# Mixer B of a two-layer trunk: where the residual's gain and shift are applied, and which engine scales the softmax rows

## The chip, the cores and the metric

The kernel runs on one core of a Trainium2 chip. The metric is the device time of one execution in microseconds (us); a lower one is better. The core has five engines that work side by side and wait for each other through semaphores: TensorE (PE in the rows; its weight loads are PEld), VectorE (DVE), ScalarE (ACT), GpSimd (POOL) and SyncE (SP), which issues the large transfers here. TensorE writes its results to PSUM, eight banks of 128 x 512 float32, which VectorE and ScalarE read; everything else lies in SBUF.

## The reference, cut to what matters

256 tokens of width 1024 in float32 pass through two layers. Layer 0 has mixer A (an mLSTM), layer 1 has mixer B (attention); after each mixer comes a mixture of 16 experts. Each of the four sub-layers ends in a layer norm over the residual:

```python
x = layer_norm(ALPHA * x + gate * f(modulate(x)), ln_g, ln_b)
# mixer B
k, v = split(modulate(x, kv_shift, kv_scale) @ w_kv)
q = modulate(x, shift, scale) @ wq / 8
p = softmax(q @ k.T - slope[h] * distance, causal)     # 16 heads of width 64
y = (p @ v) @ wo
```

## The kernel before, in words

The Python code is traced once into straight-line programs, one for each engine. Where nothing pins the order, a list scheduler decides it at build time: the priority is the order of the code, and an instruction is placed when its inputs, its buffers and its engine are free by the scheduler's own model. At run time every engine runs its list in order, so an instruction that waits holds up all behind it.

**Norm.** The norm that ends the experts of layer 0 leaves in `xt` the normalised residual without gain and shift (`normalise`, L572 to L577). Mixer B's modulations fold gain and shift into their own coefficients, so keys, values and queries need no other form of it. The residual that is added after mixer B does need it, times ALPHA: `xt = xt * (ALPHA g) + ALPHA b`. Gain and shift are rows of 1024 values. `ln_bank` (L509 to L514) makes one half of a row, the same on all 128 partitions, with a matmul into a PSUM bank. In the kernel before, `ln_rows` (L503 to L507) copies the four banks, times ALPHA, to an SBUF tile `lnrow` on ScalarE, and `ln_affine` (L579 to L582) applies them with four GpSimd operations of 128 x 1024. The call stands behind the transposes for the queries (L1491, L1492).

**Mixer B** (L1403 to L1547). The weights come in tiles of 512 KB through a ring of SBUF slots; all their loads are issued on SP's queue in the order of the code, each waiting until its slot is free. Each tile is split into two parts for precision: a cast on ScalarE (L267) and a subtraction on VectorE (L268), into one of three buffers. The products then take three matmuls each (L276 to L278). The order is `k_part(0)`, the queries' transposes, `k_part(1)`, `q_part(0)`, scores 0 and 1, `v_part(0)`, attends and scores in turn, `q_part(1)`, attends 2 and 3, scores 4 and 5, `v_part(1)`, attends 4 and 5 with scores 6 and 7, the product with `wo`, attends 6 and 7. `scores(e)` (L1445 to L1467) handles two heads: matmuls into two `bankB`, the distance term and the row maxima on VectorE, four exponentials with their sums on ScalarE, a reciprocal on VectorE, and the scaling of the rows by it. Token tile t = 0 (128 x 128 for each head) is scaled on VectorE, token tile t = 1 (128 x 256) on GpSimd (L1466). `attend(e)` transposes the rows on TensorE into two `bankB`, copies them to SBUF on ScalarE (L1478) and multiplies them with the values (L1482).

`bankA` and `bankB` are pools of four PSUM banks each. `bankB` serves the scores, the attends' transposes, the norm's rows, and the sums of the modulation's coefficients. Those sums are background work: `pump` (L433) threads the products of `w_ada` (L396, L398: VectorE, 128 x 512 each) between the splits.

Behind mixer B come the residual's addition (L558, L559), the norm, the router and the experts of layer 1 (`moe`), whose weights stream through the same ring. `moe` applies its own gain and shift from PSUM rows at L1344 and L1345, in the form the change now uses in mixer B.

Of the kernel before, what the change touches and what calls it, by code (L numbers as in the profile page):

```python
# [9 lines left out]
F32 = mybir.dt.float32  # L10
# [3 lines left out]
AF = mybir.ActivationFunctionType  # L14
OP = mybir.AluOpType
# [3 lines left out]
P = 128  # L19
D = 1024  # L20
# [11 lines left out]
ALPHA = (2.0 * 2) ** 0.25  # L32
# [120 lines left out]
def body(tc, **aps):  # L153
    with ExitStack() as ctx:
        _body(ctx, tc, **aps)


def _body(ctx, tc, x, w_ada, a_w_in, a_wq, a_wk, a_wv, a_w_out, b_w_kv, b_wq, b_wo, moe_w_gate, moe_w_up,
          moe_w_down, pc, rows, cst, out):
    nc = tc.nc  # L160
    V, A, T = [Ordered(tc, e) for e in (nc.vector, nc.scalar, nc.tensor)]
    G = nc.gpsimd
# [10 lines left out]
    def bankA(name):  # L173
        return psA.tile([P, 512], F32, tag="A", name=name)

    def bankB(name):
        return psB.tile([P, 512], F32, tag="B", name=name)
# [3 lines left out]
    xt = keep.tile([P, NT, D], F32, name="xt")  # L181
# [74 lines left out]
    def cols(w, j, name):  # L256

        v = [piece(f"{name}_{i}", w[512 * i:512 * i + 512, 512 * j:512 * j + 512]) for i in range(2)]
        return lambda k: v[k // 4][:, k % 4:k % 4 + 2, :]
# [26 lines left out]
    def dense_cm(pool, w, ks, act, banks, name, part=None):  # L286

        for i in range(0, len(ks), 2):
            if part is not None and i not in part:
                continue  # L290
            pump()
            ws = split(pool, w(ks[i]), f"{name}{ks[i]}")
            for z in range(2):
                if z:
                    pump()
                block_cm(banks, ws[z], act(i + z), i + z == 0, i + z == len(ks) - 1)

    def dense_tm(pool, w, ks, act, banks, name):

        for i in range(0, len(ks), 2):  # L300
            pump()
            ws = split(pool, w(ks[i]), f"{name}{ks[i]}")
            for z in range(2):
                if z:
                    pump()
                for t in range(NT):
                    mm3(banks[t], act(i + z, t), ws[z], i + z == 0, i + z == len(ks) - 1)
# [195 lines left out]
    def ln_rows(ln, t, scale):  # L503
        for q in range(2):
            for h in range(2):
                A.activation(t[q][:, 512 * h:512 * h + 512], ln_bank(ln, q, h, bankB), AF.Copy, scale=scale)
        return t  # L507

    def ln_bank(ln, q, h, bank):  # L509

        pg = bank(f"lnps{ln}_{q}_{h}")
        r = 8 * q + 2 * ln + h
        T.matmul(pg, pick[:, r:r + 1].to_broadcast([P, P]), lnr, start=True, stop=True)
        return pg  # L514
# [10 lines left out]
    def modulated(src, emit, name):  # L525

        for k2 in range(KD // 2):
            pt = transposed(src, name, k2)
            for kk in range(2):
                emit(2 * k2 + kk, pt[:, 256 * kk:256 * kk + 256], k2 % 2)  # L530
# [7 lines left out]
    def affine_split(hi, lo, sc, sh, nm):  # L538
        def emit(k, ps, odd):
            t = small.tile([P, S], F32, tag="cv", name=f"{nm}{k}")  # L540
            affine(t, ps, sc, sh, k, odd)
            split_to(hi[:, k, :], lo[:, k, :], t)
        return emit
# [32 lines left out]
            return A.activation(xt[:, t, :], src[:, t, :], AF.Identity, bias=nb, scale=st[1])  # L576
        return V.tensor_scalar(xt[:, t, :], src[:, t, :], st[0], st[1], op0=OP.subtract, op1=OP.mult)  # L577

    def ln_affine(row):  # L579
        for t in range(NT):  # L580
            G.tensor_tensor(xt[:, t, :], xt[:, t, :], row[0], op=OP.mult)
            G.tensor_tensor(xt[:, t, :], xt[:, t, :], row[1], op=OP.add)  # L582


    actx = ExitStack()
# [819 lines left out]
    pbh = bctx.enter_context(tc.tile_pool(name="pbh", bufs=1, reuse_waits="tile"))  # L1405
# [25 lines left out]
    def v_part(i):  # L1431
        w = cols(b_w_kv, 2 + i, f"wv_{i}")
        banks = [bankA(f"bv{i}_{t}") for t in range(NT)]
        dense_tm(wsp, w, range(KD), lambda k, t: (kh[:, k, P * t:P * t + P], kl[:, k, P * t:P * t + P]), banks, f"bv{i}_")
        for t in range(NT):
            A.copy(vv[:, t, 512 * i:512 * i + 512], banks[t])

    def q_part(i):
        w = cols(b_wq, i, f"wq_{i}")
        banks = [bankA(f"bq{i}_{c}") for c in range(2)]  # L1440
        dense_cm(wsp, w, range(KD), lambda k: (qh[:, k, :], ql[:, k, :]), banks, f"bq{i}_")
        for c2 in range(2):
            V.tensor_scalar(qs[(2 * i + c2) % QZ], banks[c2].rearrange("p (a b) -> p a b", a=2), 0.125, None, op0=OP.mult)

    def scores(e):  # L1445

        q = qs[(e // 2) % QZ]
        sb = pb3.tile([P, 2, 384], F32, tag="sb", name=f"sb{e}")
        ps = [bankB(f"s{2 * e + par}") for par in range(2)]
        for t in range(NT):  # L1450
            for par in range(2):
                r = slice(64 * par, 64 * par + 64)
                T.matmul(ps[par][:, P * t:P * t + P + P * t], q[r, e % 2, P * t:P * t + P], kT[r, e, 0:P + P * t], start=True, stop=True)
        for par in range(2):
            V.scalar_tensor_tensor(sb[:, par, :], dist, -(2.0 ** (-8.0 * (2 * e + par + 1) / AH)), ps[par][:, 0:384],
                                   op0=OP.mult, op1=OP.add)
        mx = small.tile([P, NT, 2], F32, tag="mx", name=f"mx{e}")
        sm_ = small.tile([P, NT, 2], F32, tag="smx", name=f"smx{e}")
        parts = [(t, par, slice(P * t, P + S * t)) for t in range(NT) for par in range(2)]
        for t in range(NT):  # L1460
            V.tensor_reduce(mx[:, t, :], sb[:, :, P * t:P + S * t], axis=AX.X, op=OP.max, negate=True)
        for t, par, c in parts:
            A.activation(sb[:, par, c], sb[:, par, c], AF.Exp, bias=mx[:, t, par:par + 1], accum_out=sm_[:, t, par:par + 1])
        V.reciprocal(sm_, sm_)
        for t, par, c in parts:
            (G if t else V).tensor_scalar(sb[:, par, c], sb[:, par, c], sm_[:, t, par:par + 1], 0.0, op0=OP.mult, op1=OP.add)  # L1466
        return sb  # L1467

    def attend(e, sb, bank=bankA):
        po = bank(f"bo{e}")  # L1470
        pT = []
        for par in range(2):
            h = 2 * e + par
            pt = bankB(f"bp{h}")
            for i in range(3):
                T.transpose(pt[:, P * i:P * i + P], sb[:, par, P * i:P * i + P], ident)
            pT.append(work[0].tile([P, 384], F32, tag="pT", name=f"bpT{h}"))
            A.copy(pT[par], pt[:, 0:384])  # L1478
        for t in range(NT):
            for par in range(2):  # L1480
                h = 2 * e + par
                T.matmul(po[64 * par:64 * par + 64, P * t:S], vv[:, t, 64 * h:64 * h + 64], pT[par][:, S * t:S + P * t],  # L1482
                         start=(t == 0), stop=(t == NT - 1))
        A.copy(oh_[:, e, :], po[:, 0:S])
        V.tensor_tensor(ol_[:, e, :], po[:, 0:S], oh_[:, e, :].bitcast(F32), op=OP.subtract)
# [2 lines left out]
        queue((8, 9, 10, 11), RATE[2])  # L1488
        k_part(0)
    modulated(xt, affine_split(qh, ql, scq, shq, "affq"), "tq")  # L1490
    lnrow = pbh.tile([P, 2, D], F32, tag="oh", name="lnrow")  # L1491
    ln_affine(ln_rows(1, [lnrow[:, q, :] for q in range(2)], ALPHA))  # L1492
    oh_ = pbh.tile([P, KD, S], F32R, tag="oh", name="oh_")
    ol_ = pbh.tile([P, KD, S], F32R, name="ol_")
    k_part(1)
    q_part(0)
    sb = {}
    sb[0] = scores(0)
    sb[1] = scores(1)
    v_part(0)  # L1500
    attend(0, sb[0])
    sb[2] = scores(2)
    attend(1, sb[1])
    sb[3] = scores(3)
    q_part(1)
    ptq.close()
    attend(2, sb[2])
    attend(3, sb[3])
    sb[4] = scores(4)
    sb[5] = scores(5)  # L1510
    v_part(1)
    attend(4, sb[4])
    sb[6] = scores(6)
    attend(5, sb[5])
# [75 lines left out]
```

## Time and profile before

| | |
|---|---|
| Time, median of 3 runs | 930.84 us (929.8 to 932.74) |
| Profiled execution, its own time | 929.63 us |
| Span of that execution (first to last instruction) | 927.9 us |
| Granted TensorE clock, mean | 0.989 of full speed |
| Busy: TensorE, VectorE, ScalarE, GpSimd | 887.9, 529.0, 334.9, 30.4 us |
| Moved from HBM | 318.56 MB, 343 GB/s over the span |

Times in the rows are microseconds from the start of the span. A matmul's record overlaps the next one's, so a run of matmuls is read by the distance of their starts. An idle time in square brackets names what ended it.

### The profile page before, as it was taken

Reading aid. Unit: us, or ns where it says so; the run is one execution under the profiler, and the core shown is the slowest. Engines: PE = TensorE matmul, PEld = TensorE weight load, DVE = VectorE, ACT = ScalarE, POOL = GpSimd, SP = SyncE. Lnnn points to the kernel's source line nnn. Section 1 sums busy time; section 2 is a strip of 40 time slices with the busy share of each in tenths; the row PEclk is TensorE's granted clock in tenths of the full one; section 3 lists DMA queues with packets and bytes.
Section 4 is the critical chain, followed back from the end, with each engine's and each line's share of the span. In section 5 each row is a group of like instructions: output and inputs, shape, how many; then the busy total and the mean of one; then the engine's idle time right before and its main releaser. Section 6 shows DMA issues by size and latency. Waiting matters only on the chain.

```text
span 927.9 us, 13867 instructions
## 1 busy us (share of the span) xinstructions
PE 887.9 (96%) x5205; PEld 542.0 (58%) x5208; DVE 529.0 (57%) x1016; ACT 334.9 (36%) x558; POOL 30.4 (3%) x42
## 2 busy tenths in 40 slices
PE   9999999999999899999999888999988999999994
PEld 5876988886867544434343268887664343434332
DVE  2475985866868843233333289998876223334317
ACT  3466665466547311111111035565552111101120
POOL 0020000000000000000000004021100000000000
PEclk9999999999999999999999999999999999999998
DMA  9999795696986989999999999967986999999993
GB/s 331 383 377 405 225 306 181 212 399 209 352 299 213 393 339 406 407 407 406 407 407 407 383 403 370 340 225 225 374 322 254 404 407 407 407 407 407 407 399 124
DMA packets 174250, 318.56 MB, mean 343 GB/s; under 512 B 10144, under 2 KB 28224, under 8 KB 174176
## 3 DMA queue, kind: packets, MB, share of 16 engines
q1 hardware_dynamic: 174032, 317.40, 92.3%
q8 instruction: 43, 0.70, 0.3%
q14 instruction: 31, 0.25, 0.1%
q10 hardware_dynamic: 144, 0.20, 0.1%
HBM read 316.51 MB, written 1.05 MB: 342 GB/s over the span
## 4 chain that ended last, share of the span: by engine, by line
PE 37%; DMA 10%; DVE 6%; issue 1%; ACT 1%; DVEq 0%; ACTq 0%; SPq 0%
PE pg L135 8%; PE py L135 7%; PE pu L135 7%; DMA w<-in_moe_w_up_dram 4%; PE ga L135 3%; PE po L135 3%; DMA w<-in_moe_w_down_dram 2%; DVE adacc L398 1%; DMA w<-in_moe_w_gate_dram 1%; PE bo L1482 1%; DMA wq<-in_b_wq_dram 1%; DMA ada<-in_w_ada_dram 1%; PE by L276 1%; PE bv L276 1%; PE by L278 1%
## 5 line engine op out<-in xcount | busy, mean ns | idle before, releaser
L135 PE MATMUL py<-w,aT 128*64 128x512 f32 (+1 forms) x576 | 117.3, 547 | 1.8 <-DMA w<-in_moe_w_down_dram 1.8
L1247 DVE SCALAR_TENSOR_TENSOR yl<-py,wsl,yh 128x512 fp32r<-128x512 f32 x28 | 21.0, 750 | 171.4 <-ACT yh L1246 171.4
L135 PE MATMUL pu<-w,xe 128*64 128x512 f32 x512 | 118.5, 596 | 0.2 <-DMA w<-in_moe_w_up_dram 0.2
L135 PE MATMUL pg<-w,xe 128*64 128x512 f32 x512 | 116.1, 597 | 0.0
L398 DVE SCALAR_TENSOR_TENSOR adacc<-ada,pk,adacc 128x512 f32<-128x512 f32 x112 | 86.0, 777 | 0.8
L135 PEld LDWEIGHTS py<-w,aT 128*64 128x64 f32 x576 | 41.2, 137 | 73.5 <-issue 59.8
L135 PEld LDWEIGHTS pu<-w,xe 128*64 128x64 f32 x512 | 36.0, 137 | 67.3 <-issue 60.6
L135 PEld LDWEIGHTS pg<-w,xe 128*64 128x64 f32 x512 | 34.8, 137 | 63.9 <-issue 58.9
L1213 ACT COPY aT<-aT 128x512 f32<-128x512 f32 x16 | 9.4, 586 | 139.5 <-PE aT L135 139.5
L558 DVE TENSOR_TENSOR lntmpe<-po,gate 128x512 f32<-128x512 f32 x56 | 36.0, 683 | 41.1 <-PE po L135 41.1
L1246 ACT ACTIVATE yh<-py,wsl 128x512 fp32r<-128x512 f32 x28 | 19.2, 687 | 84.0 <-PE py L135 84.0
L536 ACT ACTIVATE xe<-ga,coef 128x256 f32<-128x256 f32 x32 | 16.1, 561 | 71.8 <-PE ga L135 71.8
L276 PE MATMUL z<-hh,wz 128*128 128x256 f32 x128 | 37.6, 294 | 0.0
L277 PE MATMUL z<-hl,wz 128*128 128x256 f32 x128 | 36.0, 281 | 0.0
L559 DVE TENSOR_TENSOR xt<-xt,lntmpe 128x512 f32<-128x512 f32 x56 | 36.0, 681 | 0.0
L278 PE MATMUL z<-hh,wz 128*128 128x256 f32 x128 | 35.9, 280 | 0.0
L135 PE MATMUL ga<-onehot,xh 128*128 128x256 f32 x128 | 31.6, 324 | 0.2
L1206 DVE TENSOR_TENSOR a<-a,pu 128x512 f32<-128x512 f32 x16 | 11.0, 688 | 36.1 <-PE pu L135 20.2
L135 PE MATMUL xm<-hh,win 128*128 128x256 f32 x144 | 28.8, 289 | 0.7 <-ACT hh L135 0.7
L135 PEld LDWEIGHTS ga<-onehot,xh 128*128 128x128 f32 x128 | 25.1, 222 | 6.0 <-DVE xt L559 4.1
L1201 ACT ACTIVATE a<-pg 128x512 f32<-128x512 f32 x16 | 9.6, 597 | 52.2 <-PE pg L135 52.2
L135 PE MATMUL ga<-onehot,xl 128*128 128x256 f32 x128 | 27.4, 280 | 0.0
(389 smaller groups left out, 1965.4 us busy)
## 6 DMA issues: line engine op xcount, KB each, us to landing
w<-in_moe_w_gate_dram SPq DMA_DIRECT2D x128, 512.0 KB, 10.2
w<-in_moe_w_up_dram SPq DMA_DIRECT2D x128, 512.0 KB, 10.2
w<-in_moe_w_down_dram SPq DMA_DIRECT2D x128, 512.0 KB, 10.2
ada<-in_w_ada_dram SPq DMA_DIRECT2D x112, 512.0 KB, 7.0
win<-in_a_w_in_dram SPq DMA_DIRECT2D x16, 512.0 KB, 8.4
wz<-in_a_w_in_dram SPq DMA_DIRECT2D x16, 512.0 KB, 5.8
wout<-in_a_w_out_dram SPq DMA_DIRECT2D x16, 512.0 KB, 6.8
wv<-in_a_wv_dram SPq DMA_DIRECT2D x8, 512.0 KB, 5.5
```

Source lines behind the costliest of these rows:

```text
L135: return self.tc.keep_in_program_order(f(*a, **kw))
L276: T.matmul(ps, l[0], r[0], start=start, stop=False, skip_group_check=True)
L277: T.matmul(ps, l[0], r[1], start=False, stop=False, skip_group_check=True)
L278: T.matmul(ps, l[1], r[0], start=False, stop=stop, skip_group_check=True)
L398: V.scalar_tensor_tensor(a, w[:, k, :], c, a, op0=OP.mult, op1=OP.add)
L536: A.activation(dst, ps, AF.Identity, bias=sh[:, k:k + 1], scale=sc[:, k:k + 1])
L558: V.tensor_tensor(tmp, y, gate[:, c], op=OP.mult)
L559: V.tensor_tensor(dst[:, t, c], dst[:, t, c], tmp, op=OP.add)
L1201: A.activation(a, pg, AF.Silu)
L1206: V.tensor_tensor(a, a, pu, op=OP.mult)
L1246: A.activation(yh, py, AF.Copy, scale=wsl[:, b:b + 1])
L1247: V.scalar_tensor_tensor(yl, py, wsl[:, b:b + 1], yh.bitcast(F32), op0=OP.mult, op1=OP.subtract)
```

## The change

In mixer B the residual's gain and shift are no longer copied to SBUF and applied on GpSimd. VectorE applies them straight from the PSUM banks, with eight operations of 128 x 512 in place of four of 128 x 1024; the factor ALPHA is taken in the same operations. This is done in two halves of the columns, the first behind `q_part(1)`, the second behind `v_part(1)`. The softmax rows of token tile t = 1 are scaled on ScalarE; those of t = 0 stay on VectorE, where the addition of 0.0 is dropped.

```diff
-    def ln_affine(row):
+    def ln_affine(h):
+
+        c = slice(512 * h, 512 * h + 512)
+        pg, pb_ = [ln_bank(1, q, h, bankB) for q in range(2)]
         for t in range(NT):
-            G.tensor_tensor(xt[:, t, :], xt[:, t, :], row[0], op=OP.mult)
-            G.tensor_tensor(xt[:, t, :], xt[:, t, :], row[1], op=OP.add)
+            V.scalar_tensor_tensor(xt[:, t, c], xt[:, t, c], ALPHA, pg, op0=OP.mult, op1=OP.mult)
+            V.scalar_tensor_tensor(xt[:, t, c], pb_, ALPHA, xt[:, t, c], op0=OP.mult, op1=OP.add)
...
         for t, par, c in parts:
-            (G if t else V).tensor_scalar(sb[:, par, c], sb[:, par, c], sm_[:, t, par:par + 1], 0.0, op0=OP.mult, op1=OP.add)
+            if t:
+                A.activation(sb[:, par, c], sb[:, par, c], AF.Copy, scale=sm_[:, t, par:par + 1])
+            else:
+                V.tensor_scalar(sb[:, par, c], sb[:, par, c], sm_[:, t, par:par + 1], None, op0=OP.mult)
...
     modulated(xt, affine_split(qh, ql, scq, shq, "affq"), "tq")
-    lnrow = pbh.tile([P, 2, D], F32, tag="oh", name="lnrow")
-    ln_affine(ln_rows(1, [lnrow[:, q, :] for q in range(2)], ALPHA))
     oh_ = pbh.tile([P, KD, S], F32R, tag="oh", name="oh_")
...
     q_part(1)
+    ln_affine(0)
     ptq.close()
...
     v_part(1)
+    ln_affine(1)
     attend(4, sb[4])
```

## Rows read from the trace of the kernel before

**Rows 1.** The page's first part: busy time, share, instructions of each engine.
```profile
PE 887.9 (96%) x5205; PEld 542.0 (58%) x5208; DVE 529.0 (57%) x1016; ACT 334.9 (36%) x558; POOL 30.4 (3%) x42
```

**Rows 2.** The chain that ended last, 690 to the end: start, length, what.
```profile
855.59 3.22 PE pg L135 x15
858.81 10.22 DMA w<-in_moe_w_up_dram
```

**Rows 3.** What SP's queue waited for, 697 to 720: total, times, longest.
```profile
SPq L226 <- PE pg L135: 15.9, 6, 13.0
```

**Rows 4.** What TensorE waited for, 552 to 686: total, times, longest.
```profile
PE bk L278 <- DVE bk L268: 2.5, 1, 2.5
PE s L1453 <- DVE qs L1443: 1.2, 1, 1.2
PE bo L1482 <- ACT bpT L1478: 0.8, 3, 0.3
```

**Rows 5.** Busy time by stretch: length, then PE, PEld, DVE, ACT, POOL, clock, DMA.
```profile
566.00:578.00 12.00, 10.28 (x79) 8.97 (x77) 12.00 (x8) 5.61 (x11) 10.72 (x4) 1.00 0.95 368
...
630.00:648.00 18.00, 18.00 (x98) 12.98 (x96) 16.05 (x29) 10.91 (x28) 3.41 (x4) 1.00 0.63 199
648.00:666.00 18.00, 17.66 (x94) 12.64 (x93) 16.35 (x29) 10.53 (x28) 2.42 (x4) 1.00 1.00 350
666.00:686.00 20.00, 19.88 (x110) 14.13 (x110) 14.32 (x33) 7.03 (x14) 0.00 (x0) 1.00 0.88 335
```

**Rows 6.** GpSimd's timeline at the norm: start, length, instruction, count.
```profile
566.28 5.67 POOL L581 TENSOR_TENSOR xt<-xt,lnrow 128x1024 f32<-128x1024 f32 x2 [411.85 <-ACT lnrow L506]
571.90 5.10 POOL L582 TENSOR_TENSOR xt<-xt,lnrow 128x1024 f32<-128x1024 f32 x2
```

**Rows 7.** VectorE's timeline around it and at the first queries.
```profile
563.63 1.40 DVE L398 SCALAR_TENSOR_TENSOR adacc<-ada,pk,adacc 128x512 f32<-128x512 f32 x2
564.96 0.74 DVE L273 TENSOR_TENSOR ql<-affq,qh 128x256 fp32r<-128x256 f32 x2
...
567.67 2.00 DVE L398 SCALAR_TENSOR_TENSOR adacc<-ada,pk,adacc 128x512 f32<-128x512 f32 x1
569.59 5.19 DVE L273 TENSOR_TENSOR ql<-affq,qh 128x256 fp32r<-128x256 f32 x2
574.71 2.84 DVE L398 SCALAR_TENSOR_TENSOR adacc<-ada,pk,adacc 128x512 f32<-128x512 f32 x1
577.47 1.21 DVE L268 TENSOR_TENSOR bk<-wk,bk 128x1024 fp32r<-128x1024 f32 x1
...
596.24 1.28 DVE L1443 TENSOR_SCALAR qs<-bq 128x512 f32<-128x512 f32 x2
```

**Rows 8.** TensorE's timeline: a norm's row among the keys; the queries' last matmul.
```profile
565.06 0.50 PE L513 MATMUL lnps<-lnr,pick 128*128 128x512 f32 x1
565.39 0.28 PE L276 MATMUL bk<-kh,bk 128*128 128x256 f32 x1
...
595.05 0.28 PE L278 MATMUL bq<-qh,bq 128*128 128x256 f32 x1
```

**Rows 9.** Line L1344's instructions: least, median, longest ns, first and last start.
```profile
L1344 DVE SCALAR_TENSOR_TENSOR xt<-xt,lnps x8: 674/678/681, 325.5 to 707.6; 128x512 f32<-128x512 f32 x8
```

**Rows 10.** Line L506's instructions, the copies of the norm's rows, same columns.
```profile
L506 ACT ACTIVATE lnrow<-lnps x8: 593/598/632, 564.4 to 884.9; 128x512 f32<-128x512 f32 x8
```

**Rows 11.** ScalarE's groups by shape, 597 to 690: busy us, mean ns, idle before.
```profile
L1463 ACT ACTIVATE sb<-sb,mx 128x256 f32<-128x256 f32 x16 | 7.9, 496 | 0.0
...
L1484 ACT CAST oh__5453<-bo 128x256 fp32r<-128x256 f32 x8 | 3.0, 372 | 4.8 <-PE bo L1482 4.8
```

**Rows 12.** GpSimd's groups, 597 to 690, same columns.
```profile
L1466 POOL TENSOR_SCALAR sb<-sb,smx 128x256 f32<-128x256 f32 x16 | 11.8, 748 | 71.4 <-DVE smx L1464 53.3 <-PE bv L278 13.6 <-PE bq L278 3.2
```

**Rows 13.** VectorE's groups of splits by shape, 597 to 690, same columns.
```profile
L268 DVE TENSOR_TENSOR bv<-wv,bv 128x1024 fp32r<-128x1024 f32 x6 | 7.7, 1279 | 0.0
...
L268 DVE TENSOR_TENSOR bq<-wq,bq 128x1024 fp32r<-128x1024 f32 x4 | 4.8, 1213 | 0.0
```

## The prediction

> **What bounds the kernel now.** I read from the end backwards. TensorE is busy for 96% of the span [rows 1], which alone says little, so the chain that ended last comes first: up to 858 us it is TensorE in the experts of layer 1, then their weight transfers [rows 2]. A gain in mixer B could be lost on those transfers. But SP's queue waited 15.9 us, once for 13.0, for the gate matmuls of these experts [rows 3]: when they begin, the ring is full and the transfers stand still. The stream to the end starts with those matmuls, so what mixer B saves arrives at the end in full.
>
> Next, TensorE's own waits inside mixer B, from 552 to 686 us. They are 2.5 us for one split of the keys' weights, 1.2 us for the first queries, and three short ones that sum to 0.8 us for the copies in the attends [rows 4]. That is 4.5 us in 134. The view that is easily misread is the busy time by stretch: VectorE shows 12.00 us busy of 12 from 566 to 578 [rows 5], as if it were the bound. Its records there are stretched. While GpSimd applies gain and shift in four operations of some 2.7 us [rows 6], VectorE finishes one operation for each of GpSimd's: the background product takes 2.00 and 2.84 us where two take 1.40 just before, and two subtractions of 128 x 256 take 5.19 where two take 0.74 [rows 7]. From the start at 567.67 to the split at 577.47 pass 9.8 us for two products and two subtractions, worth about 1.40 + 0.74 less overlap, 2.0 us by the earlier rows. **VectorE lost 7.8 us there; TensorE lost 2.5**, because it still had keys to multiply when the split came late. That difference is the case.
>
> **The change, part by part.** All sums are made against the profiled execution, 929.63 us (span 927.9 and 1.73 around it). The median of the runs is 930.84, 1.21 above it; I carry the difference over to the median.
>
> *GpSimd's four operations go.* VectorE's 7.8 us go with them. On the path only TensorE's wait of 2.5 us disappears: the split of L268 stood behind the stretched operations and would be done some 7 us sooner, before TensorE wants it. Minus 2.5 us, with bounds from 0 (the split is then late for another reason, its cast on ScalarE say) to 2.5.
>
> *The wait of 1.2 us for the first queries.* The scaling of the queries starts at 596.24 [rows 7] while the queries' last matmul ends near 595.33 (595.05 and 0.28 [rows 8]); VectorE was working off its delay. It starts at once if VectorE is not behind. I take 0.9 us (596.24 less 595.33); bounds 0 and 1.2.
>
> *The four matmuls of the norm's rows move.* Among the keys each displaces its neighbour by 0.33 us [rows 8], together 1.3. They leave a stretch where TensorE is full and enter another like it, behind `q_part(1)` and `v_part(1)`: net 0. The four ScalarE copies of 0.60 us [rows 10] go (four of the eight belong to the last norm and stay): worth nothing on the path, as the casts they delayed led to the same late split.
>
> *Eight VectorE operations come.* The same form, from PSUM, takes 678 ns [rows 9]: 5.4 us, in two groups of four. VectorE's idle time from 630 to 686 is 1.95 + 1.65 + 5.7 = 9.3 us [rows 5], so they fit; behind them stand splits of `wv` and `wo`, which have three buffers, so that VectorE may run up to three tiles ahead of TensorE. That lead hides a group of 2.7 us; taken at nothing. Without it each group costs its 2.7 us.
>
> *The softmax scaling moves to ScalarE.* Sixteen operations of 128 x 256. No row has this one; the cast of that shape takes 372 ns and the exponential, which also has an operand for each row, 496 [rows 11]. The exponential is the closer: 16 x 0.496 = 7.9 us (6.0 at the lower end). GpSimd took 748 ns each [rows 12], so a row is ready sooner. ScalarE is busy for 10 to 11 us in each stretch of 18 [rows 5] and has room, but it is the engine whose copies the attends wait for. The Trainium skill, page "ScalarE: Activation LUTs", section "Rules for kernel authors", speaks against this: multiplications belong on VectorE, not on ScalarE. By it the sixteen would go to VectorE and ScalarE would be left as it was; the sum below would then hold only half of its last term. The rows weigh otherwise: VectorE is the fuller of the two, and the work comes from GpSimd.
>
> *What is new on the path.* The PSUM rows hold two of the four `bankB` until the last of four VectorE operations, while attends and scores on either side want two each; and the attends' copies now stand behind scalings on ScalarE. Lower bound 0: the scheduler can put value or output matmuls into the gaps, as it does now. Upper bound: TensorE stands for both groups, 2 x 2.7 = 5.4 us, and for what is queued ahead of them on VectorE. I take as much again as TensorE now loses to the attends' copies, 0.8 us, since these gaps are the nearest thing to it.
>
> *Small gains in the scores.* VectorE's splits of `wv` average 1279 ns, those of `wq` 1213 [rows 13]: 6 x 0.066 = 0.4 us that GpSimd's scalings cost VectorE. It is not on the path: zero. The Trainium skill, page "SBUF — State Buffer", section "Who interferes with whom", says that a VectorE instruction with two SBUF inputs and a GpSimd instruction that reads SBUF exclude each other for the whole instruction. At the norm the rows agree; in the scores that rule would allow up to 11.8 us of GpSimd time to be taken from VectorE, and these rows show 0.4. The sum by the one or the other is the same, as TensorE does not wait there.
>
> **Sum:** -2.5 - 0.9 + 0 + 0.8 = -2.6 us: 927.0 for the profiled execution, 928.2 for the median.
>
> **The rivals.** About 0.3%, 2.8 us, is what a measurement of this kernel can tell from no change.
>
> *No new wait.* The scheduler fills every gap; then the 3.4 us stay, and up to 1.1 more of the present waits go: -3.4 to -4.5, about 927.1 at its middle. For it: today 0.8 us of waits in all attends. Against it: two banks fewer for a while.
>
> *VectorE is the bound.* If TensorE's full rows were only waiting in disguise, all 7.8 us would come back: 923.0. For it: VectorE at 12 of 12. Against it: TensorE shows 10.28 us busy of those 12, and only 4.5 us of waiting in all of mixer B are there to be removed.
>
> *The gain is eaten, or does not arrive.* The new waits take 1.5 to 6.2 us, or the last transfers are late for their own reasons: 929 to 933.6, around 930.8. For it: a full ring is no proof that each later tile shifts.
>
> *Slower: the held banks.* VectorE takes the two groups behind what is queued on it, the queries' scaling, a product and a split (0.6 + 0.7 + 1.1 = 2.4 us), and TensorE, without banks for attends or scores, stands. Price: 2 x 2.7 = 5.4 to 2 x 5.1 = 10.2 us; with half the queue 2 x 3.9 = 7.8, less the 3.4 gained: +4.4, 935.2. It decides once TensorE waits over 6.2 us at the two places. For it: VectorE is 16.05 us busy of 18 where the first group falls [rows 5]. Against it: the order can put value matmuls, which use `bankA`, there.
>
> **How the numbers follow.** The forecast, -1.9 to -3.3, has 0.40, and lies across the 2.8 us line: 0.17 faster, 0.23 same. No new wait 0.22 and VectorE as the bound 0.07: faster. Gain eaten 0.18: same. Held banks 0.13: slower. Faster 0.46, same 0.41, slower 0.13. The range leaves out VectorE as the bound and the held banks, 0.20: its lower end is the best case, -4.5 and 0.7 for the scatter of the runs, 925.6; its upper end the start of the slower case, 933.6.
>
> **What would show it.** Right: VectorE's subtractions for the queries at 0.4 us, no wait of TensorE for the split of the keys near 576; the score matmuls some 3 us sooner; the gate matmuls of layer 1 2 to 3 us sooner, and the last transfer by the same. The new operations near 0.68 us, the scalings near 0.5. Wrong: TensorE's wait for the split still there (another cause than GpSimd), a gate start that moved while the end did not (the transfers have their own limit), or TensorE waiting for banks held by the two groups (then the sum's last term was too small).

## The result, and the profile after

The kernel after takes 924.45 us in the median of 6 runs (924.04 to 926.37); the kernel before, run beside it, 929.9. The ratio is 0.994, with a 95% interval of 0.9925 to 0.9956: 5.5 us faster, 3.75 us below the forecast and 1.15 below its range. The profiled execution of after took 924.04 us (span 922.4), 5.6 less than that of before.

The page's first part, as in [rows 1]:

```profile
PE 886.3 (96%) x5205; PEld 541.8 (59%) x5208; DVE 523.7 (57%) x1024; ACT 339.1 (37%) x570; POOL 7.9 (1%) x22
```

GpSimd loses 22.5 us of busy time. VectorE has eight instructions more and is nevertheless 5.3 us less busy: the records that GpSimd had stretched are short again, and the sixteen softmax scalings that stay with it take 281 ns each where they took 363. Shares of the span say nothing of the gain: TensorE is at 96% in both.

**The place where it was expected.** The same 12 us as in [rows 5], then lines of VectorE's timeline from that stretch and the start of the queries' scaling, as in [rows 7]:

```profile
566.00:578.00 12.00, 12.00 (x101) 11.35 (x100) 11.96 (x22) 7.76 (x14) 0.00 (x0) 1.00 1.05 406
```

```profile
567.68 0.73 DVE L398 SCALAR_TENSOR_TENSOR adacc<-ada,pk,adacc 128x512 f32<-128x512 f32 x1
568.40 0.76 DVE L273 TENSOR_TENSOR ql<-affq,qh 128x256 fp32r<-128x256 f32 x2
569.08 1.22 DVE L268 TENSOR_TENSOR bk<-wk,bk 128x1024 fp32r<-128x1024 f32 x1
...
573.24 1.22 DVE L268 TENSOR_TENSOR bq<-wq,bq 128x1024 fp32r<-128x1024 f32 x1
...
589.72 1.41 DVE L1446 TENSOR_SCALAR qs<-bq 128x512 f32<-128x512 f32 x2 [0.57 <-PE bq L278]
```

VectorE is still busy for all but 0.04 us of the stretch, but with 22 instructions in place of 8. The pair of subtractions that took 5.19 us takes 0.76. The last split of the keys begins between 569 and 570, where in [rows 7] it began at 577.47, and `wq` is being split at 573. The scaling of the first queries now waits for TensorE, no longer the other way round. TensorE is at 12.00 of 12, where it was 10.28.

**TensorE's waits**, from 552 to 686 us, all of them, as in [rows 4]:

```profile
PE bo L1488 <- ACT bpT L1484: 2.2, 4, 0.9
PE pr L1012 <- ACT xT L1008: 0.2, 1, 0.2
```

The waits for the keys' split (2.5) and the first queries (1.2) are gone; those for the attends' copies grew from 0.8 to 2.2 us.

**The new place.** VectorE at the first half of the norm, and TensorE there:

```profile
621.51 0.74 DVE L398 SCALAR_TENSOR_TENSOR adacc<-ada,pk,adacc 128x512 f32<-128x512 f32 x1
622.17 1.28 DVE L1446 TENSOR_SCALAR qs<-bq 128x512 f32<-128x512 f32 x2
623.37 1.27 DVE L584 SCALAR_TENSOR_TENSOR xt<-xt,lnps 128x512 f32<-128x512 f32 x2
624.56 1.28 DVE L585 SCALAR_TENSOR_TENSOR xt<-lnps,xt 128x512 f32<-128x512 f32 x2
```

```profile
621.96 0.63 PE L513 MATMUL lnps<-lnr,pick 128*128 128x512 f32 x2
622.43 0.82 PE L1482 MATMUL bp<-cs,sb 128*128 128x128 f32 x6
623.64 1.25 PE L1488 MATMUL bo<-bpT,bv 128*64 128x256 f32 x8 [0.40 <-ACT bpT L1484]
624.82 0.87 PE L1482 MATMUL bp<-cs,sb 128*128 128x128 f32 x6
```

The group of four takes 2.5 us from 623.37, and TensorE works through it. Its one wait there, 0.40 us, is for ScalarE's copy of an attend, not for a bank that the rows hold. The two matmuls push their follower back by 0.47 us (621.96 to 622.43); two pairs cost 0.95.

The new operations by shape, busy time and mean, from 591 to 685 us: VectorE's two forms, then ScalarE's scaling.

```profile
L585 DVE SCALAR_TENSOR_TENSOR xt<-lnps,xt 128x512 f32<-128x512 f32 x4 | 2.6, 682 | 0.0
L584 DVE SCALAR_TENSOR_TENSOR xt<-xt,lnps 128x512 f32<-128x512 f32 x4 | 2.5, 679 | 0.0
```

```profile
L1470 ACT ACTIVATE sb<-sb,smx 128x256 f32<-128x256 f32 x16 | 7.2, 500 | 0.8 <-DVE smx L1467 0.8
```

Both prices taken from neighbouring rows hold: 680 ns for the 678 of [rows 9], 500 for the 496 of [rows 11].

**Where the time came from.** Each value below is a start or an end of matmuls in TensorE's timeline, counted from the first transpose of the keys (`tk`, at 546.58 in before and in after), which takes out most of what differs between executions ahead of mixer B (what it leaves in is said under the next table). The first score is the first matmul into `s`; the output ends with the last product with `wo`; the gate is the first gate matmul (`pg`) of layer 1.

| us from the first `tk` | keys end | first score | output ends | gate starts | span ends |
|---|---|---|---|---|---|
| before | 35.1 | 50.4 | 139.2 | 158.8 | 381.4 |
| after | 30.7 | 44.7 | 134.7 | 153.3 | 375.8 |
| difference | -4.4 | -5.7 | -4.5 | -5.5 | -5.6 |

From the gate to the end it is 222.5 us in both: what mixer B and the router save arrives in full. Of the 5.5 us, 5.7 are there at the first score, 1.2 are lost again in the attends, and 1.0 come in the stretch from the output to the gate, 19.7 us before and 18.6 in after, which the prediction did not look at.

### The profile page after: what moved, and what is told of

Read it like the earlier page. It is cut to its first block, busy times and chain, and to the rows that moved or that the text cites. A ratio compares the mean times of both kernels' runs of the same rounds, so it can differ in the third digit from the quotient of the medians.

```text
span 922.4 us, 13836 instructions
## 1 busy us (share of the span) xinstructions
PE 886.3 (96%) x5205; PEld 541.8 (59%) x5208; DVE 523.7 (57%) x1024; ACT 339.1 (37%) x570; POOL 7.9 (1%) x22
## 4 chain that ended last, share of the span: by engine, by line
PE 42%; DMA 8%; DVE 3%; ACT 1%; issue 0%; DVEq 0%; SPq 0%; ACTq 0%
PE py L135 8%; PE pg L135 8%; PE pu L135 7%; DMA w<-in_moe_w_up_dram 3%; PE po L135 3%; PE ga L135 3%; DMA w<-in_moe_w_down_dram 2%; DMA w<-in_moe_w_gate_dram 1%; PE bo L1488 1%; DMA ada<-in_w_ada_dram 1%; PE by L276 1%; PE bq L276 1%; PE bk L277 1%; PE bk L278 1%; PE bk L276 1%; PE by L278 1%
## 5 line engine op out<-in xcount | busy, mean ns | idle before, releaser
L398 DVE SCALAR_TENSOR_TENSOR adacc<-ada,pk,adacc 128x512 f32<-128x512 f32 x112 | 82.6, 747 | 0.7
```

The source lines that it names most:

```text
L398: V.scalar_tensor_tensor(a, w[:, k, :], c, a, op0=OP.mult, op1=OP.add)
```

## The experiments

The question was which part of the change the 5.5 us come from: GpSimd's four operations, by way of VectorE (the theory), or the four row matmuls that left the keys, the late place of the work, the softmax scaling on ScalarE, or the router behind it (the rivals). The table has the same five points for all kernels; ratios are against runs of before on the same chip.

| kernel | ratio (95%) | keys end | first score | output ends | gate starts | span ends |
|---|---|---|---|---|---|---|
| norm only (e1) | 0.9944 (0.9931 to 0.9958) | 30.7 | 44.7 | 134.5 | 154.2 | 376.3 |
| softmax only (e2) | 1.0001 (0.9991 to 1.0011) | 36.2 | 50.4 | 140.1 | 159.9 | 382.3 |
| before without GpSimd's norm (e3) | 0.9957 (0.9943 to 0.9971) | 32.8 | 46.4 | 135.1 | 154.7 | 377.3 |
| after without the norm (e4) | 0.9944 (0.9929 to 0.9959) | 30.7 | 44.7 | 133.2 | 152.8 | 375.1 |
| after, norm at the old place (e5) | 0.9985 (0.9971 to 0.9999) | 32.1 | 46.1 | 138.1 | 158.0 | 380.2 |
| before with half of GpSimd's norm (e6) | 0.9951 (0.9938 to 0.9964) | 32.7 | 46.3 | 135.1 | 154.6 | 377.0 |
| after, once more (e7) | 0.9937 (0.9922 to 0.9951) | 30.7 | 44.7 | 134.7 | 153.6 | 376.0 |
| after, rows made early (e8) | 0.9947 (0.9934 to 0.996) | 33.1 | 48.1 | 136.5 | 155.3 | 377.8 |
| after, router filled (e9) | 0.9925 (0.9912 to 0.9939) | 31.1 | 45.2 | 135.1 | 153.2 | 375.9 |
| before, router filled (e10) | 0.9993 (0.9981 to 1.0005) | 36.3 | 50.4 | 139.2 | 157.6 | 380.2 |

One difference between executions stays in these counts. In most of the traces the granted clock is 0.50 around the first `tk`, and how far behind it this slow stretch reaches differs: 5.6 to 5.8 us in e3, e5, e6 and e9, 4.3 us or less in the others. The rows from 550 to 552 in before and in e3 (the clock is the third column from the right), and then the 17th product of the keys in each:

```profile
550.00:552.00 2.00, 1.53 (x13) 1.29 (x12) 2.00 (x5) 0.06 (x1) 0.00 (x0) 1.00 1.05 407
550.00:552.00 2.00, 2.00 (x13) 1.99 (x12) 1.98 (x6) 0.60 (x2) 0.00 (x0) 0.59 1.05 406
```

```profile
553.00 0.28 PE L277 MATMUL bk<-kl,bk 128*128 128x256 f32 x1
552.82 0.28 PE L277 MATMUL bk<-kl,bk 128*128 128x256 f32 x1
```

It starts 6.4 us behind the first `tk` in before and 6.9 in e3. In e5, e6 and e9 it is 6.8 to 6.9, in the others 6.4 (8.2 in e8, which waits there for its own reason). So 0.4 to 0.5 us have to be taken off the points of e3, e5, e6 and e9 before they are compared with the rest.

### The change in its two parts (e1, e2)

e1 is before with the norm of after alone, e2 before with the softmax scaling alone:

```diff
-    lnrow = pbh.tile([P, 2, D], F32, tag="oh", name="lnrow")
-    ln_affine(ln_rows(1, [lnrow[:, q, :] for q in range(2)], ALPHA))
...
     q_part(1)
+    ln_affine(0)
...
     v_part(1)
+    ln_affine(1)
```

```diff
-            (G if t else V).tensor_scalar(sb[:, par, c], sb[:, par, c], sm_[:, t, par:par + 1], 0.0, op0=OP.mult, op1=OP.add)
+            if t:
+                A.activation(sb[:, par, c], sb[:, par, c], AF.Copy, scale=sm_[:, t, par:par + 1])
+            else:
+                V.tensor_scalar(sb[:, par, c], sb[:, par, c], sm_[:, t, par:par + 1], None, op0=OP.mult)
```

> The change's norm part alone: gain and shift on VectorE from PSUM rows in two late halves; the softmax rows of token tile 1 stay on GpSimd. Theory A (the gain is TensorE's waits that GpSimd's four norm operations caused, plus the place of the low-clock stretch in the router): the wait for the keys' split and for the first queries go, the first score matmul stands near 591.3 us as in the changed kernel, and the time is 4 to 6 us below before. Rival B (half or more comes from the softmax's move): 2 to 3 us below before.

> The change's softmax part alone: token tile 1 scaled on ScalarE; the norm stays on GpSimd at its old place. Theory A: TensorE still waits about 2.5 us for the keys' split and 1.2 us for the queries; the attends' waits for ScalarE's copies grow from 0.8 to about 2; time between 1.5 us below and 2 us above before. Rival B: 2 to 3 us below before.

Measured: e1 925.07 us, ratio 0.9944; e2 930.57, ratio 1.0001. TensorE's waits in e2, from 552 to 686:

```profile
PE bk L278 <- DVE bk L268: 2.5, 1, 2.5
PE bo L1485 <- ACT bpT L1481: 1.5, 3, 1.0
PE s L1453 <- DVE qs L1443: 0.2, 1, 0.2
```

The norm carries the gain; the softmax part by itself is worth nothing either way, to 1 us. In e2 the wait for the keys' split is there as before, and the attends' copies are waited for 0.7 us longer. The wait for the first queries is 1.0 us shorter, but that is no gain: in this execution the granted clock fell to 0.50 (580 to 582) behind the wait for the split, the keys end 1.1 us later than in before, and the first score stands at the same 50.4. The Trainium skill, page "ScalarE: Activation LUTs", section "Rules for kernel authors", puts multiplications on VectorE; here 16 of them on ScalarE, at 0.50 us each, cost the kernel nothing that can be measured; they were not tried on VectorE.

### GpSimd's operations alone, all and half (e3, e6)

e3 is before without GpSimd's four operations; the rows are still made and copied. It leaves out gain and shift of mixer B's residual. e6 keeps the two multiplications, and leaves out the shift.

```diff
-    ln_affine(ln_rows(1, [lnrow[:, q, :] for q in range(2)], ALPHA))
+    ln_rows(1, [lnrow[:, q, :] for q in range(2)], ALPHA)
```

```diff
-            G.tensor_tensor(xt[:, t, :], xt[:, t, :], row[1], op=OP.add)
```

> The kernel before without GpSimd's four norm operations: the rows are still made and copied to SBUF, but gain and shift of that residual are left out. Theory A: VectorE's two subtractions for the queries take 0.74 us instead of 5.19, the 2.5 us wait for the keys' split and most of the 1.2 us wait for the queries go, the first score matmul moves from 597.0 to 593 or 594 (the rows' matmuls still stand among the keys), and the time falls by 3 to 5 us. Rival C (VectorE is the bound): it falls by 7 us or more. Rival D (the split is late for another reason): it does not fall.

> The kernel before with only the two multiplications on GpSimd; the shift of that residual is left out. GpSimd is busy there for about 5.4 us instead of 10.7. Theory A (TensorE had some 5 us of keys in hand, so a loss of VectorE up to that size costs it nothing): VectorE loses about 4 us, TensorE's wait for the keys' split is under 0.5 us, and the time is close to that without any GpSimd norm, 3 to 4 us below before. Rival G (the loss is passed on in proportion): half of that gain, about 2 us below before.

Measured: e3 926.35 us, 0.9957; e6 925.59, 0.9951. Both are 4.0 to 4.1 us earlier than before, at the first score and at the end of mixer B's output; with the slow clock at the keys taken off (0.5 us in e3, 0.4 in e6) it is 4.5 in both, at both points. In e6 GpSimd and VectorE look like this:

```profile
567.01 5.49 POOL L581 TENSOR_TENSOR xt<-xt,lnrow 128x1024 f32<-128x1024 f32 x2 [411.42 <-ACT lnrow L506]
```

```profile
568.23 1.99 DVE L398 SCALAR_TENSOR_TENSOR adacc<-ada,pk,adacc 128x512 f32<-128x512 f32 x1
570.14 2.97 DVE L273 TENSOR_TENSOR ql<-affq,qh 128x256 fp32r<-128x256 f32 x2
573.04 0.74 DVE L398 SCALAR_TENSOR_TENSOR adacc<-ada,pk,adacc 128x512 f32<-128x512 f32 x1
573.70 1.21 DVE L268 TENSOR_TENSOR bk<-wk,bk 128x1024 fp32r<-128x1024 f32 x1
```

TensorE's waits in mixer B are a single line in e6 (552 to 680, up to the last output matmul), and e3's list from 552 to 680 has the same one alone:

```profile
PE bo L1481 <- ACT bpT L1477: 0.8, 3, 0.3
```

With half of GpSimd's work VectorE still loses about 3.5 us (4.96 for one product and two subtractions that take 1.5 elsewhere), and **the kernel loses none of it**: the last split ends at 574.9, before TensorE has run out of keys. The price is not a share of what VectorE loses; it begins when TensorE's stock of split tiles is used up. That is the prediction's reading of [rows 4 to 7], and e3 and e6 together show it. The Trainium skill, page "SBUF — State Buffer", section "Who interferes with whom", has it that a VectorE instruction with two SBUF inputs and a GpSimd instruction that reads SBUF exclude each other. The rows of e6 agree for the norm: while GpSimd's two operations run, to 572.5, VectorE's product and its subtractions are stretched, and from 573.04 all are short again.

### The norm left out of after (e4)

After without the two calls, so without the eight VectorE operations and the four row matmuls; it leaves out gain and shift of that residual.

```diff
-    ln_affine(0)
...
-    ln_affine(1)
```

> The changed kernel without the norm's eight VectorE operations and four matmuls (gain and shift of that residual are left out): the price of the two late halves. Theory A (only the four matmuls cost, about 0.33 us each, VectorE's eight are hidden): 1 to 1.6 us below the changed kernel, or 6 to 7 us below before. Rival E (the held banks or VectorE's 5.4 us are paid on the path): 3 us or more below the changed kernel.

Measured: 924.76 us, 0.9944, within the interval of after; the times do not show the 1 to 1.6 us that were expected. The trace shows what the four matmuls cost at either place, up to the end of the output. Against e3, which has them among the keys, e4 ends the output 1.9 us sooner, 1.5 with e3's slow clock taken off. Against after, which has them among the attends, it is 1.5 us too; 0.95 of that is the four matmuls themselves, and the rest, 0.6, goes with the longer waits for the attends' copies (2.2 against 1.1). No wait of TensorE is put down to the eight VectorE operations; if they cost anything by way of those copies, it is within this 0.6. e4 is also without the four ScalarE copies of the rows; no wait in e3's list is put down to ScalarE's work on the keys.

### The same work early on VectorE (e5)

```diff
+    ln_affine(0)
+    ln_affine(1)
     oh_ = pbh.tile([P, KD, S], F32R, tag="oh", name="oh_")
...
     q_part(1)
-    ln_affine(0)
...
     v_part(1)
-    ln_affine(1)
```

> The changed kernel with both halves of the norm at the old place, behind the queries' transposes, on VectorE. It tells how much the late place is worth. Theory A (VectorE has little idle time among the keys, so its 5.4 us delay splits there, but no more than TensorE can cover in part): the end of mixer B 1 to 3 us later than in the changed kernel, time 2 to 4 us below before. Rival F (the place does not matter, only that GpSimd is silent): within 0.5 us of the changed kernel.

Measured: 928.44 us, 0.9985 (0.9971 to 0.9999). TensorE's waits, 552 to 686:

```profile
PE bp L1482 <- DVE sb L1458: 1.9, 1, 1.9
PE bo L1488 <- ACT bpT L1484: 0.9, 3, 0.4
PE bp L1482 <- DVE sb L1472: 0.4, 1, 0.4
```

So taking the work from GpSimd is not enough. With the eight operations before the scores, the first score is still 4.3 us earlier than before, but between the end of the first values' product and the start of the second queries 10.4 us pass where after needs 6.8. TensorE's transposes wait there for VectorE's work on the scores (`sb`). That it is the norm's operations that make it late was not tried apart. Behind that wait the granted clock falls, too: the row from 610 to 612, and then eight score matmuls before the fall and eight in it.

```profile
610.00:612.00 2.00, 2.00 (x13) 1.30 (x12) 1.98 (x4) 1.68 (x4) 0.00 (x0) 0.53 0.71 238
```

```profile
605.35 0.93 PE L1456 MATMUL s<-bkT,qs 64*128 64x128 f32 x8
611.34 1.66 PE L1456 MATMUL s<-bkT,qs 64*128 64x128 f32 x8
```

At the end of the output e5 is 3.4 us behind after (138.1 against 134.7), 2.9 with the slow clock at the keys taken off, and a part of that is this second slow stretch. The times say the same of the place: 0.9985 against 0.9937 for after on the same chip (e7), with intervals that do not overlap.

### Rows made early, applied late (e8)

After, but the rows are made before the keys' transposes, copied to two SBUF slots by ScalarE, and applied by VectorE from there at the late places.

```diff
+    rowB = room("lnrowB", 2)
+    ln_rows(1, rowB, ALPHA)
...
-        pg, pb_ = [ln_bank(1, q, h, bankB) for q in range(2)]
...
-            V.scalar_tensor_tensor(xt[:, t, c], xt[:, t, c], ALPHA, pg, op0=OP.mult, op1=OP.mult)
-            V.scalar_tensor_tensor(xt[:, t, c], pb_, ALPHA, xt[:, t, c], op0=OP.mult, op1=OP.add)
+            V.tensor_tensor(xt[:, t, c], xt[:, t, c], rowB[0][:, c], op=OP.mult)
+            V.tensor_tensor(xt[:, t, c], xt[:, t, c], rowB[1][:, c], op=OP.add)
```

> The changed kernel with the four rows made ahead of the keys' transposes, where TensorE waits 3.3 us for the norm of the experts, and copied on ScalarE into two slots of the weights' ring; VectorE's eight operations stay late and read SBUF. Theory A (the rows' matmuls cost about 0.33 us each wherever TensorE is full): the end of mixer B about 1.3 us earlier than in the changed kernel, time 6 to 7 us below before. Rival H (the two ring slots or ScalarE's four copies ahead of the keys' casts cost as much): no better than the changed kernel.

Measured: 925.16 us, 0.9947. TensorE's waits from 552 to 682:

```profile
PE bk L277 <- DVE kl L273: 1.6, 1, 1.6
PE bp L1483 <- DVE sb L1459: 1.1, 1, 1.1
PE bo L1489 <- ACT bpT L1485: 0.5, 2, 0.3
```

The attends are cleaner (0.5 us of waits for the copies in place of 2.2, and the output 88.4 us behind the first score instead of 90.0), but the keys pay for it: a wait of 1.6 us for their own split, one of 0.9 us before 552 for ScalarE's cast of `kh`, and keys that end 2.4 us later than in after. (The first score is 3.5 us later, but e8 has four more of the first values' matmuls ahead of it, 0.9 us; so the 88.4 flatters it by as much.) So it is no better than after. ScalarE makes these copies in the stretch in which it casts the keys; that this is what delays them was not tried apart.

### After once more (e7), and the way to the gate

> The changed kernel once more, unaltered. From the last matmul of mixer B to the first gate matmul it took 18.6 us in its profile and 19.6 to 19.8 in the five others, with the stretch at half clock lying earlier. If that belongs to the kernel, it is 18.6 again; if it is the chance of one execution, it can be 19.7, and the profiled time 1 us longer.

Measured: 924.05 us, 0.9937. The five points repeat to 0.3 us, the gathers described below less well (5.2 us here, 4.8 in after). That left the stretch from the output to the gate, 18.6 and 18.9 us in the two executions of after, 19.5 to 19.9 in before and in e1 to e6. Busy time by stretch, with the granted clock as third column from the right; first before, then after:

```profile
698.00:700.00 2.00, 1.48 (x10) 0.61 (x9) 1.88 (x12) 0.00 (x0) 0.00 (x0) 0.97 1.00 388
700.00:702.00 2.00, 1.94 (x10) 1.91 (x10) 2.00 (x7) 0.37 (x1) 0.00 (x0) 0.50 0.45 174
702.00:704.00 2.00, 2.00 (x14) 2.00 (x14) 1.32 (x4) 1.11 (x2) 0.00 (x0) 0.68 0.11 43
```

```profile
692.00:694.00 2.00, 0.28 (x6) 0.24 (x6) 1.87 (x18) 0.47 (x1) 0.00 (x0) 0.80 1.06 409
694.00:696.00 2.00, 2.00 (x7) 1.12 (x6) 1.96 (x9) 0.00 (x0) 0.00 (x0) 0.50 1.05 407
696.00:698.00 2.00, 2.00 (x16) 2.00 (x16) 2.00 (x8) 1.06 (x1) 0.00 (x0) 0.84 0.63 241
```

In the router TensorE stands still for the experts' mask, 3.45 us in before and 4.43 in after, and then its granted clock is 0.50, which is the lower of its two levels, 1.2 GHz. In before that stretch lies over the 32 gather matmuls (`ga`, from 699.68), which take 5.73 us up to the gate; in after about half of it is over before they begin at 695.16, and they take 4.77. Both kernels fill such pauses with matmuls that nobody reads (`stay_warm`), five here; e9 and e10 make them twenty, in both layers, in after and in before.

```diff
-WARM = 5, 4
+WARM = 20, 4
```

> The kernel after, with 20 instead of 5 filling matmuls ahead of each layer's routing: TensorE stands still 4.4 us there in layer 1 and 3.4 us in layer 0, and 15 more of 0.25 us fill most of that. Theory (about 1 us of the change's gain is where the stretch at a granted clock of 0.50 falls behind that pause, across the first gather matmuls): with no pause there is no such stretch, the 32 first gather matmuls take 32 x 0.12 = 3.8 us in both layers instead of 5.9 (layer 0) and 4.8 (layer 1); the way from mixer B's last output matmul to layer 1's first gate matmul is 17.6 to 17.9 instead of 18.6, and the time is 921.0 to 922.0. Rival (the 1 us is the order of the router's instructions alone): the way stays 18.4 or more and the time 924 to 925. If the filling runs past the mask that ends the wait, the way is over 19 and the time over 925.

> The kernel before with the same 20 filling matmuls. Theory: the first gather matmuls take 3.8 us instead of 5.9 and 5.7, the way from mixer B's last output matmul to layer 1's first gate matmul falls from 19.7 to about 17.8, the time to 926.0 to 927.0; against the filled kernel after that is a difference of 4.5 to 5.0 us, where the unfilled pair differs by 5.5 to 5.9. Rival (order alone): 930 or more, the way stays 19.5 or more, and the difference to the filled kernel after stays 5.5 to 5.9 us.

Measured: e9 923.43 us (922.59 to 924.38), e10 929.03 (927.61 to 931.46). First e9's, then e10's rows:

```profile
694.00:696.00 2.00, 1.50 (x10) 0.61 (x9) 1.88 (x12) 0.00 (x0) 0.00 (x0) 1.00 1.05 408
696.00:698.00 2.00, 2.00 (x17) 2.00 (x17) 2.00 (x7) 0.40 (x1) 0.00 (x0) 1.00 0.80 310
```

```profile
698.00:700.00 2.00, 1.61 (x11) 0.63 (x10) 1.90 (x12) 0.00 (x0) 0.00 (x0) 1.00 0.93 361
700.00:702.00 2.00, 2.00 (x17) 2.00 (x17) 2.00 (x8) 0.48 (x1) 0.00 (x0) 1.00 0.43 166
```

The clock stays at 1.00 in both, the way to the gate falls to 18.1 and 18.4 us, and the difference between the two kernels on it from 1.0 to 0.3. In these traces the theory holds: some 0.7 us of the difference is where a slow stretch falls. Its sizes were too large: the 32 matmuls take 4.3 and 4.4 us from the first gather to the gate, not 3.8. And **the times do not decide it**. Each of the two medians lies between the numbers of the theory and those of the rival. Between them lie 5.6 us, which is within the rival's 5.5 to 5.9 and not the theory's 4.5 to 5.0; the profiled pair differs by 4.3 from the first `tk` to the end, 4.8 with e9's slow clock at the keys taken off. The intervals of the ratios are 0.0027 and 0.0024 wide, over 2 us each, so the times cannot tell 0.7 us. e9 has the lowest median of all; its interval overlaps with that of after, so it is not shown to be faster than after.

The gathers alone do not give the way. In e2, whose router has the order of before's, the slow stretch came earlier, from 692 on:

```profile
692.00:694.00 2.00, 2.00 (x19) 1.01 (x14) 0.15 (x1) 1.88 (x3) 0.00 (x0) 0.50 1.05 407
698.00:700.00 2.00, 0.65 (x7) 0.37 (x7) 1.84 (x18) 0.00 (x0) 0.00 (x0) 0.50 0.97 377
```

Its gathers take 4.7 us, but the mask comes 1.0 us later behind the output than in before, and the way is 19.8 us: there the slow clock is paid ahead of the gathers.

## Why the prediction was wrong

The direction, the cause and the path were right, the size was not: -2.6 us was forecast for the profiled execution, -5.6 came (-5.5 up to the gate). The step that failed is **the price of GpSimd's operations, taken from TensorE's list of waits**: 3.4 us, with a bound of 3.7, where e3 and e6 show 4.5. Two more went the same way: the new waits, +0.8, of which nothing is left in the net, and a sum that ended at mixer B's output, where 1.0 us more came behind it. Term by term:

- *The keys' split, -2.5, and the first queries, -0.9.* Right in kind, 1.1 us too small. With GpSimd's operations alone gone (e3) the first score and the output came 4.0 us sooner, 4.5 with the slow clock at the keys taken off. In the trace these 4.5 are 2.7 around the wait for the split (the keys' last 32 products take 8.4 us in before and 5.6 in e3); 0.5 in the queries, which ran behind splits that were still late (from their first to their last matmul 13.85 us in before, 13.31 in e3, with no single wait in TensorE's list); and 1.2 between the queries and the first score, where the sum took 0.9. The view of waits gave a lower bound, and I took it for the whole.
- *The moved matmuls, net 0, and the new waits, +0.8.* Together 0.0: the output ends at 134.7 in after, and at 135.1 in e3, 134.7 with its slow clock taken off. By e4 the four matmuls cost 1.5 us at either place. Among the keys that is more than 4 x 0.33: in before the starts of the keys' products on either side of three of the rows lie 0.58 to 0.65 us apart, where 0.12 is the rule. (In e5 three rows among the keys cost less, 0.35 us from start to start, so it is not the row alone; why is open.) Late and in pairs they cost 0.95 together, and the waits for the attends' copies, which grew by 1.4 us in the list, bring it to the same 1.5.
- *The way from the output to the gate, not in the sum.* -1.0 us, the one term that I had no reason to expect from the rows I read. The traces of e9 and e10 put 0.7 of it down to the slow stretch of the clock behind the mask; the times of these runs do not decide it. Why that stretch begins at the end of the wait in after and 1.5 us later in before is open.
- *The base.* I carried 1.21 us from the profiled execution to the median of three. Over six runs before has 929.9, 0.3 above its profiled execution, and after stands 0.41 above its own. Of the 3.75 us between forecast and median, 0.8 (1.21 less 0.41) is this.

What held: what mixer B saves arrives (222.1 to 222.7 us from the gate to the end in all twelve traces); no wait is put down to the eight operations, and e4 leaves 0.6 us at most for them; the scalings cost 0.50 us each and nothing that the time of e2 shows; VectorE's splits of `wv` take 1220 ns without GpSimd's scalings (e2), as read from [rows 13]; SP's queue waits for the gate matmuls as in [rows 3], 11.4 us at the longest in after where it was 13.0.

The rivals. *No new wait* was the closest: at the output it is -4.5, its best case, though not for its reason, as waits for copies did grow. (Its middle, -3.95 from 930.84, is 926.9, not 927.1.) *VectorE is the bound* comes out near the right time (923.0), for a wrong reason: VectorE lost 3.5 us in e6 and the kernel nothing. *Held banks* did not happen; TensorE waits 0.40 and 0.87 us at the two places, both times for ScalarE's copies, not the 6.2 that would have decided. *The gain does not arrive* fell with the 222.5 us.

The range's lower end was the best case of *no new wait*, which left no room for a second gain behind mixer B; with the base at 929.9 in place of 930.84 that end would be 924.66, and it would still have missed the result, by 0.2 us.

## What to carry to other kernels

A stretched engine costs only what lies beyond the stock that its consumer still holds: half of GpSimd's work stretched VectorE by 3.5 us for nothing, all of it by 7.8 us for 4.5. The consumer's list of waits gives a lower bound of that price, so add the pauses too short to be listed, by comparing a run of like matmuls from its first start to its last with a run that had nothing to wait for. And carry the sum through to the point where the end is set: behind the part that is changed, a wait and a clock can move too. When traces of two executions are laid side by side, compare the granted clock at the point from which you count: here it put 0.5 us between kernels that did the same work.

## What the runs showed of the hardware beyond that

The way through a slow clock need not be paid by the work after the pause. In before the granted clock was still 0.97 over the two microseconds in which the wait ended (698.42) and fell to 0.50 after it; in after it was down to 0.80 over the two in which the wait ended (693.72). With the fall at either place the gathers took 5.73 and 4.77 us.

In layer 0 the filled router of e10 lets the gate matmuls start 1.5 us sooner (328.28 against 329.82), and almost nothing of it reaches mixer B, whose first transpose starts at 546.40 instead of 546.58. In e10 TensorE has a wait between 330 and 546 that before does not have:

```profile
PE po L135 <- issue: 1.7, 1, 1.7
```

e9 has the same wait, and its gate starts 1.4 us sooner than that of after with nothing gained at the first `tk`. What TensorE waits for there the profile doesn't show; that the wait swallows the gain is likely by its size and was not tested.
